# Projections' weights in a stream of their own, two dense chunks between load and split, and one conv buffer for the attention keys

## The chip, the cores and the metric

The kernel runs on one core of a Trainium2 chip. The metric is the device time of one execution in microseconds (us); lower is better. Engines are named as the profile names them: PE is TensorE's matmul and PEld its weight load, DVE is VectorE, ACT is ScalarE, POOL is GpSimd, SP is SyncE, whose queue issues nearly all transfers. A "q" behind an engine's name (SPq) is its instruction queue, where it issues transfers or waits.

## The reference

One encoder block over 2048 tokens and 16 meta tokens of width 1024. One input projection feeds two mixers, whose outputs are joined by an output projection, followed by a SwiGLU feed-forward part.

```python
def reference(x, meta_tokens, g_mix, w_in, ...):
    h = jnp.concatenate([meta, x], axis=1)
    u = rmsnorm(h, g_mix[l])
    proj = u @ w_in[l]
    na_q, na_k, na_v, dn_q, dn_k, dn_v, dn_z, dn_b, dn_a = jnp.split(proj, pts, axis=-1)
    y_na = neighbourhood_attention(na_q, na_k, na_v, na_rel_bias[l], rows)
    y_dn = gated_deltanet(dn_q, dn_k, dn_v, dn_z, dn_b, dn_a, dn_conv_w[l], ...)
    h = h + jnp.concatenate([y_na, y_dn], axis=-1) @ w_out[l]
    u = rmsnorm(h, g_ffn[l])
    h = h + (jax.nn.silu(u @ w_gate[l]) * (u @ w_up[l])) @ w_down[l]
```

`gated_deltanet` first applies a five-tap convolution over the tokens and a silu to q, k and v, then works in chunks of 64 tokens, forward and backward, each of which needs the inverse of a small triangular matrix.

## The kernel before

Three phases follow one another: `phase_a` (the input projection, the convolutions and what the DeltaNet needs before its scan), `phase_b` (attention and scan) and `phase_c` (output projection and feed-forward part). The change lies in `phase_a`, which ends near 890 us of the trace.

All products are kept near f32 accuracy by splitting: a value is `hi`, a rounded copy, plus `lo`, the rest, and a product is three matmuls (hi x hi, hi x lo, lo x hi). A weight tile therefore passes through three steps: a transfer of a raw piece (L220), a cast to `hi` on ACT (L221), a subtraction to `lo` on POOL (L222). The raw pieces share two buffers named `raw`.

`phase_a` goes twice over the units of the projection, once for each half of the tokens. A half has 20 feature units ("f": 12 blocks of DeltaNet channels, 4 pairs of heads of attention keys, 4 of queries; weight tile `wf`, three buffers, two raw pieces each) and 4 natural units ("n": `v0`, `v1`, `z0`, `z1`; tile `wn`, one buffer, four raw pieces). A feature unit is three dense chunks of 24 matmuls at L400, a natural one about eight chunks of 24 at L424. At the end of each chunk stands a tick: the side streams `post` (what follows a convolution), `pre` and `first` (the DeltaNet's chunk work) are Python generators, and each tick moves them to their next `yield`; `yield n` lets n ticks pass. At a unit's start `ahead(u)` writes the loads and splits of units u, u+1 and, where it is a feature unit, u+2.

At the end of a DeltaNet block its convolution is written: the first tap on ACT (L492), four taps on DVE (L494), into a buffer of `ct`, which has two. `post_conv` then makes the silu (Tanh on ACT, L624; product on DVE, L625), lets two ticks pass, and transposes on PE (L631). At the end of an attention key unit, `na_k` makes `hi` (L527, ACT) and `lo` (L528, DVE) of 512 columns twice, each pair in a `ct` buffer of its own, and stores each (L516).

Two loads of results that were stored to memory shortly before stand in `meta_state` (L774, the meta keys `kT`, used by PE at L781) and in `pre_unit` (the inverses' lanes, used by PE at L930). Each engine executes its own list in order; the order in the lists is the program's, with small moves that a scheduler makes.

Of the kernel before, what the change touches and what calls it, by code (L numbers as in the profile page):

```python
# [8 lines left out]
F32 = mybir.dt.float32  # L9
F32R = mybir.dt.float32r  # L10
I32 = mybir.dt.int32
AF = mybir.ActivationFunctionType
ALU = mybir.AluOpType
# [3 lines left out]
P = 128  # L17
NT = 2048
NM = 16
L = NT + NM  # L20
D = 1024
KB = 8
# [3 lines left out]
HT = NT // 2  # L26
# [16 lines left out]
def key_row(r):  # L43
    return r + (r >= 4) + (r >= 27)
# [39 lines left out]
class Side:  # L84
# [8 lines left out]
    def add(self, gen, ready=lambda: True):  # L93
        self.q.append([gen, ready, 0])

    def step(self):
        for e in list(self.q) if self.together else self.q[0:1]:
            if not e[1]():
                continue
            e[2] -= 1  # L100
            if e[2] > 0:
                continue
            try:
                e[2] = next(e[0]) or 1
            except StopIteration:
                self.q.remove(e)
                self.done += 1


class Pieces:  # L110
# [78 lines left out]
def phase_a(tc, S, x, meta, x_t, xe_t, g_mix_b, g_mix_c, w_feat, w_nat0, w_nat, conv_w, a_log, dt_bias, handover):  # L189
# [3 lines left out]
    nc = tc.nc  # L193
    with ExitStack() as es:
        early = es.enter_context(ExitStack())
        cv = early.enter_context(tc.tile_pool(name="cvA", bufs=2))
        wfp = early.enter_context(tc.tile_pool(name="wfA", bufs=3))
        upool = es.enter_context(tc.tile_pool(name="uT", bufs=1, side="right"))
        wpool = es.enter_context(tc.tile_pool(name="wA", bufs=2, side="right"))
# [12 lines left out]
        rb, gb = gb, gb[:, 0:D]  # L212
        gc_ = sm.tile([P, KB], F32, name="gc", bufs=1)
        U = Ctx()
        post, pre, first = Side(True), Side(), Side()
        behind = Behind(tc)

        def split(hi, lo, src):
            raw = wpool.tile(list(src.shape), F32, name="raw")
            nc.sync.dma_start(raw, src)  # L220
            nc.scalar.copy(hi, raw)  # L221
            nc.gpsimd.tensor_tensor(lo, raw, hi, ALU.subtract)  # L222

        def load_feat(b):
            hl = wfp.tile([P, 2, KB, P], F32R, name="wf")
            for q in range(2):
                ks = slice(q * 4, q * 4 + 4)
                split(hl[:, 0, ks], hl[:, 1, ks], w_feat[b][:, ks])
            return hl

        def load_nat(src, n):
            hl = wpool.tile([P, 2, KB, 272], F32R, name="wn", bufs=1)
            for q in range(4):
                ks = slice(q * 2, q * 2 + 2)
                split(hl[:, 0, ks, 0:n], hl[:, 1, ks, 0:n], src[:, ks])
            return hl

        rsx = sm.tile([P, 20], F32, name="rsx", bufs=1)
        nc.gpsimd.memset(rsx, 1.0)
# [126 lines left out]
                    put(job, xt, ci, half, n != 3)  # L366

        def step():
            post.step()
            pre.step()  # L370
            first.step()
# [6 lines left out]
                tick()  # L378

        units, W = [], {}  # L380

        def load(u):
            if u < len(units) and u not in W:
                kind, arg = units[u][0], units[u][1]
                W[u] = load_feat(arg) if kind == "f" else load_nat(*arg)

        def ahead(u):

            load(u)
            load(u + 1)  # L390
            if u + 2 < len(units) and units[u + 2][0] == "f":
                load(u + 2)

        def dense_feat(u, ci, c0, c1):
            hl = W[u]
# [9 lines left out]
        def run_feat(u, ci):  # L405
            kind, b, cols, evac, fin = units[u]
            c0, c1 = cols[ci]
            evac(ci, dense_feat(u, ci, c0, c1))
            tick()
            if ci == 2:  # L410
                fin()
                W.pop(u)

        def run_nat(u, ci):
            kind, (src, n), with_meta, evac, fin = units[u]
            hl = W[u]
            for r0, np_, off, is_meta in U.plan[ci]:
                if np_ == 2 or (is_meta and not with_meta):
                    continue
                ps = pacc.tile([P, 512], F32, name="acc")  # L420
                i = 0
                for k in range(KB):
                    for a, l in ((0, 0), (1, 0), (0, 1)):
                        nc.tensor.matmul(ps[0:np_, 0:n], (U.h, U.l)[l][ci][:, k, off:off + np_], hl[:, a, k, 0:n],  # L424
                                                start=(i == 0), stop=(i == 23))
                        i += 1
                evac(r0 // P, np_, is_meta, ps)
                tick()
            if ci == 2:
                W.pop(u)  # L430
                if fin:
                    fin()

# [65 lines left out]
        def na_k(hp, half):  # L499
            st = Ctx()  # L500
            st.raw = None
            cols = [(16, 400) if half == 0 else (2, 386), (0, 384), (0, 256 if half == 0 else 272)]

            def evac(ci, ps):
                if st.raw is None:
                    st.raw, st.pos = cv.tile([P, HT + NM + 4], F32, name="cr", bufs=3), 0
                n = cols[ci][1] - cols[ci][0]
                nc.scalar.copy(st.raw[:, st.pos:st.pos + n], ps[:, 0:n])
                st.pos += n

            def fin():
                raw = st.raw

                def store(hl, i):
                    n = hl.shape[2]
                    nc.sync.dma_start(S.kx[hp, :, :, :, i * 64:i * 64 + n].rearrange("l a d n -> (a d) l n"), hl.bitcast(F32))  # L516
                if half == 1:
                    m = sm.tile([P, 2, 4, NM], F32R, name="km", bufs=1)
                    mv = bc(raw[:, HT:HT + NM].rearrange("p (o c) -> p o c", o=1), [P, 4, NM])
                    nc.scalar.copy(m[:, 0], mv)  # L520
                    nc.vector.tensor_tensor(m[:, 1], mv, m[:, 0], ALU.subtract)
                    for i in META_ROWS:
                        store(m.rearrange("p l o c -> p l (o c)"), i)
                for rr in range(2):
                    khl = cv.tile([P, 2, 512], F32R, name="ct")
                    g = raw[:, rr * 512:rr * 512 + 512]
                    nc.scalar.copy(khl[:, 0], g)  # L527
                    nc.vector.tensor_tensor(khl[:, 1], g, khl[:, 0], ALU.subtract)  # L528
                    r0 = half * 16 + rr * 8
                    cut = next((c for c in (4, 27) if r0 < c < r0 + 8), r0 + 8)  # L530
                    for c0, c1 in ((r0, cut), (cut, r0 + 8)):
                        if c0 < c1:
                            store(khl[:, :, (c0 - r0) * 64:(c1 - r0) * 64], key_row(c0))
            return ("f", 12 + hp, cols, evac, fin)

        def na_q(hp, half):
# [27 lines left out]
            passes.append(unit_order(half, dn, na, v0, v1, z0, z1))  # L564
        for us in passes:
            units.extend(us)
        u0 = 0
        for pi, us in enumerate(passes):
            if pi == 0:
# [4 lines left out]
            n = len(us)  # L574
# [3 lines left out]
            for gi, grp in enumerate(groups):  # L578
# [4 lines left out]
                if pi == 0 and gi == 13:  # L583
                    first.add(row_rs())
                for i in grp:
                    ahead(u0 + i)
                for ci in range(3):
                    for i in grp:
                        run(u0 + i, ci)
# [170 lines left out]
def meta_state(tc, S, Q, cv, ptp):  # L760

    nc = tc.nc
# [10 lines left out]
    nc.sync.dma_start(gb, bc(S.growm.rearrange("(o h) i -> o h i", o=1), [NM, 4, NM]))  # L773
    nc.sync.dma_start(kT, S.mkT.rearrange("h p i -> p h i"))  # L774
    key_scale(nc, S, slice(0, NM), slice(0, 4), slice(16, 17), False)
    yield 3
    pk_ = ptp.tile([P, 4, P], F32, name="tp").rearrange("p a b -> p (a b)")
    pk = pk_[0:NM, 0:64].rearrange("p (h i) -> p h i", h=4)
    for h in range(4):
# [34 lines left out]
def pre_unit(tc, S, Q, hp, half):  # L814


    nc = tc.nc
    lane = S.lane[hp * 2 + half]
    c0 = half * 8
# [98 lines left out]
    back(ab[32:64, :, 0:32], 1, 1, 1)  # L918
    back(ab[64:96, :, 0:32], 1, 1, 2)
    back(ab[96:128, :, 32:64], 1, 1, 3)  # L920
    yield 4

    def inner(d):

# [972 lines left out]
```

## Time and profile before

| what | value |
|---|---|
| time, median of 3 runs | 2927.22 us (2924.75 to 2933.74) |
| the profiled execution, its own time | 2921.78 us |
| its span in the profile | 2920.1 us |
| PE busy | 2756.5 us (94%) |
| DVE busy | 1780.5 us (61%) |
| ACT busy | 1170.1 us (40%) |
| POOL busy | 745.8 us (26%) |
| mean granted clock of TensorE | 0.966 |

The span is what the profile covers; the time is measured around the whole execution. Busy shares are means over the three phases. Gaps in square brackets in the timeline rows below are the idle time just before an instruction and what ended it.

### The profile page before, as it was taken

To read this page: it belongs to the slowest core of one execution; us is meant where nothing else is said; L and a number is where in the kernel's file an instruction comes from. 1 tells how busy PE (TensorE), PEld (TensorE's weight loads), DVE (VectorE), ACT (ScalarE), POOL (GpSimd) and SP (SyncE) were. 2 spreads that over 40 slices of the span, in tenths; PEclk is the share of its full clock that TensorE was granted. 3 is DMA by queue.
4 is the path that set the end of the run, shared out by engine and by line. 5 is a ranking of instruction groups with operands and counts; after the bars stand their busy time and mean duration, and the time that the engine had idled before them with its cause. 6 is when DMAs were issued, how large, how long until landed. Compare 5 with 4: busy or idle time off the path is not lost.

```text
span 2920.1 us, 45810 instructions
## 1 busy us (share of the span) xinstructions
PE 2756.5 (94%) x16364; PEld 2414.9 (83%) x16364; DVE 1780.5 (61%) x3908; ACT 1170.1 (40%) x2741; POOL 745.8 (26%) x769
## 2 busy tenths in 40 slices
PE   8899989998898998979999999999999999999998
PEld 8889989988888888868887888887887888888886
DVE  5787458796563556874568565555447655554354
ACT  5652233552314666752234233333434332333342
POOL 2353243251421112241224322210014322320010
PEclk9999999999998999989999999999999999999999
DMA  5675564575759988985545222237353222225452
GB/s 160 177 196 147 141 175 122 180 193 148 203 138 281 277 239 236 306 259 182 180 134 182 78 87 82 65 112 262 132 184 111 92 87 78 81 94 193 142 178 73
DMA packets 398017, 466.32 MB, mean 160 GB/s; under 512 B 91955, under 2 KB 302220, under 8 KB 396222
## 3 DMA queue, kind: packets, MB, share of 16 engines
q1 hardware_dynamic: 396062, 457.11, 51.7%
q0 software_dynamic: 1728, 6.29, 0.6%
q8 instruction: 130, 2.13, 0.3%
q14 instruction: 97, 0.79, 0.1%
HBM read 334.14 MB, written 141.15 MB: 163 GB/s over the span
## 4 chain that ended last, share of the span: by engine, by line
PE 68%; DVE 11%; DMA 11%; issue 4%; ACT 2%; POOL 2%; SPq 1%; DVEq 0%; ACTq 0%; POOLq 0%
PE pg L1599 24%; PE pg L1675 8%; PE pd L1459 6%; PE acc L400 4%; PE pd L1675 4%; PE tp L1675 4%; PE acc L424 4%; PE pd L1599 4%; DVE ct L494 2%; PE y L1139 2%; DMA b<-in_rel_dram 2%; DMA qr<-qx 1%; DMA raw<-in_w_nat_dram 1%; DVE tl L162 1%; DVE yl L163 1%
## 5 line engine op out<-in xcount | busy, mean ns | idle before, releaser
L400 PE MATMUL acc<-uh,wf 128*128 128x384 f32 (+5 forms) x1920 | 472.7, 331 | 4.8 <-issue 3.6
L1443 DVE TENSOR_TENSOR w<-rw,w 128x512 fp32r<-128x512 f32 x308 | 244.4, 796 | 250.8 <-ACT w L1442 249.9
L1599 PE MATMUL pg<-T,w 128*128 128x512 f32 x1584 | 393.9, 397 | 1.8 <-ACT T L1442 0.9
L1599 PE MATMUL pg<-B,w 128*128 128x512 f32 x1584 | 389.1, 398 | 3.7 <-ACT B L1442 3.0
L1442 ACT CAST w<-rw 128x512 fp32r<-128x512 f32 x308 | 190.3, 620 | 485.2 <-PE tp L1675 252.2
L1599 PEld LDWEIGHTS pg<-B,w 128*128 128x128 f32 x1584 | 299.8, 190 | 78.0 <-ACT B L1442 4.0
L1599 PEld LDWEIGHTS pg<-T,w 128*128 128x128 f32 x1584 | 298.4, 189 | 75.4 <-ACT T L1442 1.6
L400 PEld LDWEIGHTS acc<-uh,wf 128*128 128x128 f32 x1920 | 342.8, 194 | 3.8 <-ACT uh L335 0.9
L400 PE MATMUL acc<-ul,wf 128*128 128x384 f32 (+5 forms) x960 | 315.1, 328 | 0.6 <-DVE ul L336 0.6
L1675 PE MATMUL pg<-w,hT 128*128 128x512 f32 x1056 | 260.9, 395 | 1.1 <-ACT hT L1442 1.1
L1547 POOL TENSOR_TENSOR s<-rw 128x512 f32<-128x512 f32 x88 | 117.3, 1334 | 548.6 <-DMA rw<-in_w_gate_dram 300.9
L1675 PEld LDWEIGHTS pg<-w,hT 128*128 128x128 f32 x1056 | 198.1, 188 | 49.9 <-ACT hT L1442 1.5
L424 PE MATMUL acc<-wn,uh 128*128 128x256 f32 (+3 forms) x1056 | 209.2, 297 | 6.4 <-DVE vs L468 6.2
L1443 DVE TENSOR_TENSOR w<-s,w 128x512 fp32r<-128x512 f32 x176 | 129.7, 740 | 133.5 <-ACT w L1442 132.3
L1442 ACT CAST w<-s 128x512 fp32r<-128x512 f32 x176 | 108.5, 620 | 234.3 <-PE pg L1599 140.5
L400 PEld LDWEIGHTS acc<-ul,wf 128*128 128x128 f32 x960 | 186.0, 194 | 5.7 <-issue 3.7
L424 PEld LDWEIGHTS acc<-wn,uh 128*128 128x128 f32 (+1 forms) x1056 | 172.5, 196 | 8.8 <-DVE vs L468 6.4
L494 DVE SCALAR_TENSOR_TENSOR ct<-cr,cw,ct 128x1024 f32<-128x1024 f32 (+1 forms) x96 | 140.6, 1467 | 40.4 <-ACT ct L492 38.9
L1459 PE MATMUL pd<-w,yh 128*128 128x512 f32 x512 | 160.0, 394 | 0.0
L424 PE MATMUL acc<-wn,ul 128*128 128x256 f32 (+3 forms) x528 | 156.1, 296 | 2.0 <-DVE rx_i L58 2.0
L222 POOL TENSOR_TENSOR wf<-raw,wf 128x512 fp32r<-128x512 f32 x80 | 110.4, 1396 | 171.7 <-ACT wf L221 154.8
L1613 DVE TENSOR_TENSOR eg<-pg,eg 128x512 f32<-128x512 f32 x110 | 75.9, 690 | 107.2 <-PE pg L1599 107.2
(358 smaller groups left out, 5337.0 us busy)
## 6 DMA issues: line engine op xcount, KB each, us to landing
rw<-in_w_down_dram SPq DMA_DIRECT2D x88, 512.0 KB
rw<-in_w_gate_dram SPq DMA_DIRECT2D x44, 512.0 KB
rw<-in_w_up_dram SPq DMA_DIRECT2D x44, 512.0 KB
hd<-eg SPq DMA_DIRECT2D x88, 256.0 KB
s<-hd SPq DMA_DIRECT2D x88, 256.0 KB
raw<-in_w_feat_dram SPq DMA_DIRECT2D x80, 256.0 KB
w<-dx SPq DMA_DIRECT2D x24, 768.0 KB
xq<-xq SPq DMA_DIRECT2D x32, 512.0 KB
```

The source lines that it names most:

```text
L222: nc.gpsimd.tensor_tensor(lo, raw, hi, ALU.subtract)
L400: nc.tensor.matmul(ps[:, 0:c1 - c0], hl[:, a, k, :], (U.h, U.l)[l][ci][:, k, c0:c1], start=(i == 0), stop=(i == 23))
L424: nc.tensor.matmul(ps[0:np_, 0:n], (U.h, U.l)[l][ci][:, k, off:off + np_], hl[:, a, k, 0:n], start=(i == 0), stop=(i == 23))
L494: nc.vector.scalar_tensor_tensor(tt, raw[:, j:j + T], cw[:, b, j:j + 1], tt, op0=ALU.mult, op1=ALU.add)
L1139: nc.tensor.matmul(po, t.pT[0:w, c], t.v[0:w, c], start=(c == 0), stop=(c == nch - 1))
L1442: nc.scalar.copy(dst_h, src)
L1443: eng.tensor_tensor(dst_l, src, dst_h, ALU.subtract)
L1459: nc.tensor.matmul(ps, (yh, yl)[a][:, k], wo[k][:, b, cs], start=(i == 0), stop=(i == 23))
L1547: nc.gpsimd.tensor_tensor(s, p, q, op)
L1599: nc.tensor.matmul(ps, w[:, a, k], t[:, b, k], start=(k == 0 and (a, b) == (0, 0)), stop=(k == 3 and a == 1))
L1613: nc.vector.tensor_tensor(dst, ps, x0, ALU.add)
L1675: nc.tensor.matmul(acc[j][hf], hk[f][:, a, j * P:(j + 1) * P], wk[f][hf][:, b], start=(f == 0 and i == 0), stop=(f == NFF - 1 and i == 2))
```

## The change

The weights get a side stream `ws` of their own. It steps first at each tick. For each unit it holds a generator that issues a pair of raw transfers, lets two ticks pass, and only then casts and subtracts both. At most three feature tiles and one natural tile are alive; a tile's place is given back at its unit's end (`gone`), and a unit whose weights are not there yet forces the stream on (`load`). `Side.step` therefore takes `force`, and goes on to the next generator in the same tick when one has ended.

`na_k` takes one `ct` buffer of 1024 columns for `hi`; `lo` is written over the raw tile; `hi` and `lo` are stored apart, two row ranges each. The two loads in `meta_state` and `pre_unit` get `yield 5` for `yield 3` and `yield 5` for `yield 4`.

```diff
-    def step(self):
-        for e in list(self.q) if self.together else self.q[0:1]:
+    def step(self, force=False):
+        for e in list(self.q):
             if not e[1]():
-                continue
+                if self.together:
+                    continue
+                return
             e[2] -= 1
-            if e[2] > 0:
-                continue
-            try:
-                e[2] = next(e[0]) or 1
-            except StopIteration:
-                self.q.remove(e)
-                self.done += 1
+            if e[2] <= 0 or force:
+                try:
+                    e[2] = next(e[0]) or 1
+                except StopIteration:
+                    self.q.remove(e)
+                    self.done += 1
+                    continue
+            if not self.together:
+                return
...
-        def split(hi, lo, src):
-            raw = wpool.tile(list(src.shape), F32, name="raw")
-            nc.sync.dma_start(raw, src)
-            nc.scalar.copy(hi, raw)
-            nc.gpsimd.tensor_tensor(lo, raw, hi, ALU.subtract)
...
+        def weights(u):
...
+            for k0 in range(0, KB, 2 * step):
+                raws = []
+                for k in (k0, k0 + step):
+                    raw = wpool.tile([P, step, n], F32, name="raw")
+                    nc.sync.dma_start(raw, src[:, k:k + step])
+                    raws.append((k, raw))
+                yield 2
+                for k, raw in raws:
+                    hi, lo = hl[:, 0, k:k + step, 0:n], hl[:, 1, k:k + step, 0:n]
+                    nc.scalar.copy(hi, raw)
+                    nc.gpsimd.tensor_tensor(lo, raw, hi, ALU.subtract)
+            W[u] = hl
...
         def step():
+            ws.step()
             post.step()
...
-                for rr in range(2):
-                    khl = cv.tile([P, 2, 512], F32R, name="ct")
-                    g = raw[:, rr * 512:rr * 512 + 512]
-                    nc.scalar.copy(khl[:, 0], g)
-                    nc.vector.tensor_tensor(khl[:, 1], g, khl[:, 0], ALU.subtract)
-                    r0 = half * 16 + rr * 8
-                    cut = next((c for c in (4, 27) if r0 < c < r0 + 8), r0 + 8)
-                    for c0, c1 in ((r0, cut), (cut, r0 + 8)):
-                        if c0 < c1:
-                            store(khl[:, :, (c0 - r0) * 64:(c1 - r0) * 64], key_row(c0))
+                hi = cv.tile([P, HT + NM], F32, name="ct")[:, 0:HT].bitcast(F32R)
+                lo = raw[:, 0:HT].bitcast(F32R)
+                nc.scalar.copy(hi, raw[:, 0:HT])
+                nc.vector.tensor_tensor(lo, raw[:, 0:HT], hi, ALU.subtract)
+                r0 = half * 16
+                cut = 4 if half == 0 else 27
+                for c0, c1 in ((r0, cut), (cut, r0 + 16)):
+                    i = key_row(c0)
+                    for l, part in enumerate((hi, lo)):
+                        nc.sync.dma_start(S.kx[hp, l, :, :, i * 64:(i + c1 - c0) * 64].rearrange("a d n -> (a d) n"),
+                                          part[:, (c0 - r0) * 64:(c1 - r0) * 64].bitcast(F32))
...
+        for u, unit in enumerate(units):
+            ws.add(weights(u), lambda u=u, k=unit[0]: u in alive[k] or len(alive[k]) < (3 if k == "f" else 1))
...
-                    ahead(u0 + i)
+                    load(u0 + i)
...
-    yield 3
+    yield 5
...
-    yield 4
+    yield 5
```

What this moves is seen in the order of the instructions. First SP's queue at the end of the first attention key unit, near 125 us of the trace; `kx` is the store of the keys, `raw` a weight's raw piece, `ab` a load for the DeltaNet's decays. Before:

```order
L516 DMA kx_57<-ct_1484 128x2x192
L516 DMA kx_57<-ct_1484 128x2x320
L835 DMA ab_1554<-grow_92 128x256
L220 DMA raw_1626<-in_w_feat_dram 128x512
L220 DMA raw_1630<-in_w_feat_dram 128x512
```

Of the change, at the same place:

```order
L521 DMA kx_57<-km_1475 128x2x64 x2
L538 DMA kx_57<-ct_1480 128x704
L538 DMA kx_57<-ct_1480 128x320
L236 DMA raw_1516<-in_w_feat_dram 128x512
L538 DMA kx_57<-cr_1363 128x704
L538 DMA kx_57<-cr_1363 128x320
L236 DMA raw_1518<-in_w_feat_dram 128x512
```

The second `ct` buffer is gone from the stores, and the pair of raw pieces stands among the stores of one key unit, no longer behind those of a second buffer.

Then ACT's list at the same place: casts of raw pieces, drains of dense chunks (L485, L490 after), the key cast (L527, L531 after) and the first tap of the next convolution (L492, L497 after). Before:

```order
L527 CAST ct_1484<-cr_1372 128x512
L634 ACTIVATE kjunk_1397,kss_1396<-tp_1457 128x128 x4
L634 ACTIVATE kjunk_1397,kss_1396<-tp_1466 128x128 x4
L485 COPY cr_1523<-acc_1567 128x384
L485 COPY cr_1523<-acc_1593 128x256
L221 CAST wf_1625<-raw_1626 128x512
L492 ACTIVATE ct_1619<-cr_1523,cw_154 128x1024
L221 CAST wf_1625<-raw_1630 128x512
```

Of the change:

```order
L531 CAST ct_1480<-cr_1363 128x1024
L642 ACTIVATE kjunk_1393,kss_1392<-tp_1457 128x128 x4
L490 COPY cr_1512<-acc_1487 128x386
L642 ACTIVATE kjunk_1393,kss_1392<-tp_1466 128x128 x4
L490 COPY cr_1512<-acc_1561 128x384
L490 COPY cr_1512<-acc_1587 128x256
L241 CAST wf_1515<-raw_1516 128x512
L241 CAST wf_1515<-raw_1518 128x512
L497 ACTIVATE ct_1617<-cr_1512,cw_154 128x1024
```

The casts now belong to a pair that was issued further ahead, and both stand before the first tap.

Last, ACT's list ahead of the last unit, `z1`: casts of its tile `wn`, drains of query units (L547, L553 after), and the first drain of `z1` itself (L467, L472 after). Before, from the last two of the four casts on:

```order
L221 CAST wn_9633<-raw_9642 128x2x256
L221 CAST wn_9633<-raw_9646 128x2x256
L547 ACTIVATE cr_9390<-acc_9467 128x4x64
L547 ACTIVATE cr_9537<-acc_9512 128x4x96
L547 ACTIVATE cr_9537<-acc_9560 128x4x96
L547 ACTIVATE cr_9537<-acc_9600 128x4x64
L547 ACTIVATE cr_9675<-acc_9650 128x4x96
L547 ACTIVATE cr_9675<-acc_9686 128x4x96
L810 COPY xt_9712<-tp_9681 128x512
L547 ACTIVATE cr_9675<-acc_9715 128x4x64
L467 ACTIVATE vs_9864<-acc_9839 128x256
```

Of the change, from the first of the four on:

```order
L241 CAST wn_9478<-raw_9479 128x2x256
L241 CAST wn_9478<-raw_9481 128x2x256
L553 ACTIVATE cr_9539<-acc_9597 128x4x64
L553 ACTIVATE cr_9650<-acc_9625 128x4x96
L241 CAST wn_9478<-raw_9592 128x2x256
L241 CAST wn_9478<-raw_9594 128x2x256
L553 ACTIVATE cr_9650<-acc_9656 128x4x96
L553 ACTIVATE cr_9650<-acc_9687 128x4x64
L818 COPY xt_9902<-tp_9791 128x512
L472 ACTIVATE vs_9952<-acc_9927 128x256
```

Before, all four casts stand ahead of seven drains of dense chunks; after, the last two stand ahead of two.

## Rows read from the trace of the kernel before

**Rows 1.** One stretch: busy PE, PEld, DVE, ACT, POOL; clock, DMA share, GB/s.

```profile
31.00:890.00 859.00, 782.85 (x6515) 760.94 (x6517) 590.67 (x1370) 344.05 (x924) 294.73 (x331) 0.94 0.60 165
```

**Rows 2.** Waits of PE in 31 to 890: total us, times, longest.

```profile
PE tp L631 <- DVE ct L625: 36.4, 11, 6.1
PE tp L781 <- DMA nat<-mkT: 7.2, 1, 7.2
...
PE pp L930 <- DMA af<-lane: 5.0, 2, 3.9
```

**Rows 3.** Waits of ACT and of SP's queue in 31 to 890.

```profile
ACT wn L221 <- DMA raw<-in_w_nat_dram: 65.1, 20, 11.8
...
ACT wf L221 <- DMA raw<-in_w_feat_dram: 39.4, 18, 7.6
...
ACT ct L527 <- DMA kx<-ct: 11.9, 4, 6.8
SPq L220 <- POOL wf L222: 89.2, 45, 12.6
```

**Rows 4.** Timelines of ACT, SP, DVE and PE, 123 to 146: start, busy us.

```profile
123.48 0.62 ACT L527 CAST ct<-cr 128x512 fp32r<-128x512 f32 x1 [3.36 <-DMA kx<-ct]
125.70 0.89 SPq L516 DMA_DIRECT2D kx<-ct  x2
127.25 3.09 SPq L220 DMA_DIRECT2D raw<-in_w_feat_dram  x2
135.40 0.62 ACT L221 CAST wf<-raw 128x512 fp32r<-128x512 f32 x1 [7.59 <-DMA raw<-in_w_feat_dram]
135.92 1.15 ACT L492 ACTIVATE ct<-cr,cw 128x1024 f32<-128x1024 f32 x1
137.11 6.22 DVE L494 SCALAR_TENSOR_TENSOR ct<-cr,cw,ct 128x1024 f32<-128x1024 f32 x4 [6.58 <-ACT ct L492]
145.17 1.11 PE L631 MATMUL tp<-ident,ct 128*128 128x128 f32 x4 [6.09 <-DVE ct L625]
```

**Rows 5.** Timelines of ACT and PE around 390, 660 and 716.

```profile
389.41 0.62 ACT L221 CAST wf<-raw 128x512 fp32r<-128x512 f32 x1 [5.21 <-DMA raw<-in_w_feat_dram]
391.98 0.75 PE L631 MATMUL tp<-ident,ct 128*128 128x128 f32 x4 [4.04 <-DVE ct L625]
658.39 0.66 PE L631 MATMUL tp<-ident,ct 128*128 128x128 f32 x4 [0.56 <-DVE ct L625]
714.04 0.62 ACT L221 CAST wn<-raw 128x512 fp32r<-128x512 f32 x1 [11.81 <-DMA raw<-in_w_nat_dram]
716.71 0.66 PE L631 MATMUL tp<-ident,ct 128*128 128x128 f32 x2 [5.39 <-DVE ct L625]
```

**Rows 6.** The chain that ended last, in order of time: start, us, what.

```profile
130.01 5.93 DMA raw<-in_w_feat_dram
213.31 9.88 PE acc L424 x83
223.19 11.49 PE acc L400 x72
699.84 14.17 DMA raw<-in_w_nat_dram
```

**Rows 7.** Groups by line and shape, 31 to 890: busy, mean ns, idle before.

```profile
L528 DVE TENSOR_TENSOR ct<-cr,ct 128x512 fp32r<-128x512 f32 x16 | 14.0, 873 | 8.9 <-ACT ct L527 8.9
L222 POOL TENSOR_TENSOR wf<-raw,wf 128x512 fp32r<-128x512 f32 x76 | 105.4, 1402 | 169.0 <-ACT wf L221 152.1 <-PE tp L631 10.6 <-PE pp L864 5.9
L222 POOL TENSOR_TENSOR wn<-raw,wn 128x512 fp32r<-128x512 f32 x24 | 36.3, 1517 | 58.5 <-ACT wn L221 53.6 <-DMA raw<-in_w_nat_dram 5.0
```

**Rows 8.** Timelines of POOL and DVE, 463 to 467.

```profile
463.32 2.84 POOL L222 TENSOR_TENSOR wf<-raw,wf 128x512 fp32r<-128x512 f32 x2 [1.83 <-ACT wf L221]
463.62 1.40 DVE L163 TENSOR_TENSOR yl<-yl,tl 128x255 f32<-128x255 f32 x1
466.48 0.42 DVE L163 TENSOR_TENSOR yl<-yl,tl 128x256 f32<-128x256 f32 x1
```

More of the change, by code (lines that the diff above doesn't have):

```diff
@@ L214, in phase_a @@
         U = Ctx()
-        post, pre, first = Side(True), Side(), Side()
+        post, pre, first, ws = Side(True), Side(), Side(), Side()
         behind = Behind(tc)
-        def split(hi, lo, src):
-            raw = wpool.tile(list(src.shape), F32, name="raw")
-            nc.sync.dma_start(raw, src)
-            nc.scalar.copy(hi, raw)
-            nc.gpsimd.tensor_tensor(lo, raw, hi, ALU.subtract)
[L224 to L236, printed above, removed]
+        def weights(u):
+            kind, arg = units[u][0], units[u][1]
+            if kind == "f":
+                hl = wfp.tile([P, 2, KB, P], F32R, name="wf")
+                n, step, src = P, 4, w_feat[arg]
+            else:
+                src, n = arg
+                hl, step = wpool.tile([P, 2, KB, 272], F32R, name="wn", bufs=1), 2
+            alive[kind].add(u)
+            for k0 in range(0, KB, 2 * step):
[10 more added lines that the diff above has]
+            W[u] = hl
         rsx = sm.tile([P, 20], F32, name="rsx", bufs=1)
@@ L380, in phase_a, with gone @@
         units, W = [], {}
+        alive = {"f": set(), "n": set()}
         def load(u):
[L383 to L392, printed above, removed]
+            while u not in W:
+                ws.step(True)
+        def gone(u):
+            W.pop(u)
+            alive[units[u][0]].discard(u)
         def dense_feat(u, ci, c0, c1):
@@ L411, in run_feat @@
                 fin()
-                W.pop(u)
+                gone(u)
         def run_nat(u, ci):
@@ L429, in run_nat @@
             if ci == 2:
-                W.pop(u)
+                gone(u)
                 if fin:
```

## The prediction

> **What bounds the kernel now.** I read first the busy time by stretch. Of the 859 us between 31 and 890, the projections' stage, TensorE works 782.85 us and is idle 76 [rows 1]; no other engine passes 591. So the stage is held by TensorE, and the change can win there only what TensorE idles, unless it makes TensorE wait for something new. Outside that stretch the two programs issue nearly the same TensorE rows in the same order, so I expect nothing there.
>
> Then the list of what TensorE waits for in that stretch [rows 2]: 36.4 us in eleven waits of the conv transposes (L631) for VectorE's silu (L625), 7.2 us in one wait for the meta keys' load (L781), 5.0 us in two waits for the lane loads (L930), together 48.6 us. No wait for a weight tile is in that list: `wf` and `wn` reach TensorE in time. The rest of the 76 us is many small waits and issue time that the change does not address.
>
> Weights nevertheless show up one step upstream. ScalarE waits 65.1 us in 20 waits at the cast L221 for raw rows of `w_nat` and 39.4 us in 18 for `w_feat`, 104.5 together; SP waits 89.2 us for GpSimd's split to free a raw buffer [rows 3]. ScalarE executes in order, so whatever is queued behind such a cast waits too. The question is how many of the eleven TensorE waits begin there.
>
> Three do, and I followed each back by time. At 145.17 TensorE has waited 6.09 us for L625. The silu comes after the five-tap conv, whose taps on VectorE (L494, from 137.11, 6.22 us in all) had waited 6.58 us for ScalarE's first tap L492 (135.92), and that stood behind a cast (135.40) that had waited 7.59 us for its raw weights. Those were only issued at 127.25, because on SP they stand behind the key store of the second `ct` buffer, whose cast L527 (123.48) had itself waited 3.36 us for an earlier key store to leave the buffer [rows 4]. At 391.98 (4.04 us) and 716.71 (5.39 us) it is shorter: the silu's Tanh L624 comes directly behind a cast that waited 5.21 us (389.41) and one that waited 11.81 us (714.04) [rows 5]. Sum of the three: 6.09 + 4.04 + 5.39 = 15.5 us.
>
> **The change, part by part.**
>
> *The casts no longer stand right behind their loads.* Before, load, cast and split of a weight are written in one go at a unit's start. After, a pair of loads is written, then two dense chunks pass, then the two casts and splits. A feature chunk takes 11.49/72 x 24 = 3.83 us, a natural one 9.88/83 x 24 = 2.86 us [rows 6], so the cover is 7.7 or 5.7 us. Raw loads that something waited for took some 6 us (5.93 at 130.01) and, once, 14.17 us [rows 6]. So most waits of a cast end, and for the three gaps I take 12 of the 15.5 us: about 1.2 us stays in each, because after the cast the chain of L492, four taps, silu still has to run, and the smallest gap of this kind, with no late cast ahead of it, is 0.56 us [rows 5]. Bounds: 0 and 15.5.
>
> *The other eight waits* sum to 36.4 - 15.5 = 20.9 us. Ahead of them VectorE is late too, but by mixed causes: casts that waited earlier for weights, the key units' `ct` pair, and VectorE's own queue with the inversion (L162, L163) between the taps. I take half, 10.4; bounds 0 and 20.9, no row decides between them.
>
> *The attention keys.* One 1024-wide cast and one 1024-wide subtraction replace two of each 512 wide, and `lo` is written over the raw tile; so a key unit takes one `ct` buffer and not two, and the 11.9 us that L527 waits for key stores [rows 3] should go. Its worth in TensorE time lies in the gap at 145 already counted. VectorE's part was 16 x 873 ns = 14 us [rows 7] and cannot become more than that. Four stores go out per unit instead of three, 8 more in all; two of them held SP for 0.89 us [rows 4], and SP has waits of 89 us to lose. I cost it at nothing, under cover of SP's idle time; without the cover it is 8 x 0.5 = 4 us.
>
> *The yields.* The meta keys' load gets two more ticks before its products. In program order the distance grows only from 0.42 to 0.96 of a chunk, since ticks in the last groups pass without dense work: 0.54 x 2.86 = 1.5 us of the 7.2. The lane loads' distance to L930 is the same in both orders, though a dense chunk now stands between L930's products and what follows. I take 4 of 7.2 + 5.0 = 12.2; bounds 1.5 and 12.2.
>
> *What the new distance costs.* The same two chunks come off the other side. Counted in program order from a tile's last split to TensorE's first use, a feature unit had about 5 chunks in hand (3.5 to 14) and now has about 2; a natural one had 3.6 to 6.3 and now has 0.8 to 2.0; two units of the second half (`v0` and the fourth conv block) have none. The rows of ScalarE before `z1` show it: all four casts of `wn` ahead of seven drains before, the last two with two drains behind them after. If one load is as late as the 14.17 us one, it lies 14.17 - 5.7 = 8.5 us past its cover, less a reserve of about one chunk of 2.86, some 6 us of TensorE; the two units without reserve cost about a split (1.5 us, [rows 7]) each. I take 9; bounds 0 (the list before has no such wait) and 28 (seven of the eight natural units late by 4 us each, a landing of 14 against cover and reserve being rare, one of 6 to 10 not).
>
> **Sum.** -12 - 10.4 - 4 + 9 = -17.4 us. The profiled execution took 2921.8 us (span 2920.1), so 2904.4; it stands 5.4 us under the median of the runs shown, 2927.2, and so I forecast 2909.8, **2910**. Its own range, with 5 us either way on the eight waits and 6 on the late weights, is about 8 us either way, 2902 to 2918.
>
> **The rivals.**
>
> *VectorE is late for a reason that stays (2924).* The transposes wait for VectorE, and the 100 splits on GpSimd in the stretch are as many and as long as before: 105.4 + 36.3 us [rows 7]. A subtraction of VectorE's inversion, 128 x 255, took 1.40 us at 463.62 beside a pair of splits running from 463.32 for 2.84 us, and one of 128 x 256 took 0.42 us at 466.48, after them [rows 8]. If such stretching makes the silu late, moving the splits by two chunks only moves the collision. By the rows: a third of the 22.4 us of the first two terms remains (7.5), the yields give 4, the new distance costs 9, so -3: 2924. Against it: in the three largest gaps the step before is an idle ScalarE, not a stretched VectorE. The Trainium skill, "SBUF — State Buffer", section "Who interferes with whom", says that a DVE instruction with two SBUF inputs and a GpSimd instruction that reads SBUF exclude one another; the trace agrees (1.40 against 0.42), and the taps and the silu have two such inputs. By that rule alone none of the first 22.4 us would come, and the time would be about 2932.
>
> *Weights arrive late (2942, slower).* The place is the start of the natural units: TensorE at L429 (the old L424) behind the last split of `wn`. It decides when a pair's casts come more than about 2.5 us after their turn, which is what one nat chunk of reserve leaves after a split; before, 20 such casts waited 65.1 us, 3.3 us each on average, and the longest 11.81. Seven units by 4 us are 28, half of the 26.4 us of gains still comes (13), so +15: 2942. Against it: half of those 3.3 us are covered by the two chunks, and TensorE waits for no weight before.
>
> *All of it closes (2878).* The eleven waits, the meta keys' and the lanes' go, and no weight is late: 48.6 us less, 2878.6. For it: every one of these waits ends with VectorE or a load, and both have time to spare. Against it: the smaller waits have no cast ahead of them.
>
> **How the numbers follow.** Chances: forecast 0.53, VectorE late anyway 0.25, late weights 0.16, all closes 0.06. A difference of 0.3%, 8.8 us, is what a measurement of this kernel can tell from no change. The forecast and the last case are faster by more, 0.59; the first rival lies within it, 0.25; the second is slower, 0.16. Leaving out the second rival's upper part and the last case, the range is 2888 (the forecast with the eight waits gone whole and no late weight, 2890, and 2 us more of the three gaps) to 2932 (the first rival with nothing of the first two terms).
>
> **What would show it.** The casts' waits for raw fall from 104.5 to under 40 us; TensorE's waits for the silu fall from 36.4 to about 14; the meta keys' wait falls from 7.2 to about 5. If the casts' waits fall and TensorE's waits for the silu do not, the first rival is right. If TensorE waits for `wf` or `wn` appear in the list with more than 15 us, the second is. I am wrong, too, if the time moves outside 31 to 890.

## The result and the profile after

The changed kernel takes 2906.51 us (median of 5 runs, 2900.0 to 2912.7) against 2927.35 for the kernel before: ratio 0.9925, interval 0.9903 to 0.9947. The forecast was 2910 in 2888 to 2932. The profiled execution has a span of 2898.0 us, 22.1 less than before.

Where the time came from is read by stage. The windows below end with the last dense chunk of the projections' stage; columns are the window, its length, then busy time (and count) of PE, PEld, DVE, ACT, POOL, then granted clock, share of the transfer engines, GB/s. First the kernel before:

```profile
31.00:898.50 867.50, 791.35 (x6599) 769.17 (x6600) 592.21 (x1373) 346.00 (x928) 298.22 (x333) 0.94 0.61 166
```

The changed kernel:

```profile
31.00:884.00 853.00, 788.46 (x6602) 765.59 (x6603) 588.06 (x1367) 347.13 (x924) 305.53 (x334) 0.95 0.62 169
```

The stage is 14.5 us shorter. TensorE's idle time in it is 11.6 us less (76.15 before, 64.54 now), and its busy time 2.9 us less, at a granted clock of 0.95 and not 0.94. The other 7.6 us lie behind the stage. There the two kernels issue the same matmuls, but not all in the same order. A second profile of the same changed kernel (run again below) is 2.8 us longer there than the first, so part of those 7.6 us is spread; I do not claim them for the change. In the kernels below the time behind the stage goes from 2010 to 2033 us, though no experiment edits a line of it. A difference in the whole time is therefore not yet a difference in the stage, and the stage's end is given with the ratio where it matters.

TensorE's waits in 31 to 890 after (total us, times, longest), the answer to [rows 2]:

```profile
PE tp L639 <- DVE ct L633: 15.9, 9, 4.0
PE pp L938 <- DMA af<-lane: 11.5, 3, 6.3
PE acc L429 <- DVE vs L473: 10.3, 2, 7.5
...
PE acc L405 <- POOL wf L242: 0.9, 1, 0.9
...
PE tp L789 <- DMA nat<-mkT: 0.6, 1, 0.6
```

The silu waits fell from 36.4 to 15.9 us and the meta keys' from 7.2 to 0.6, together 27.1. The lanes' waits rose, from 5.0 to 11.5, and so did the products of a natural unit that wait for VectorE to drain the one before (L429, L424 before), from 6.2 to 10.3. This is most of why 27.1 us less of the first two came to only 11.6 us less idle time. A wait for a weight is now there, but it is one of 0.9 us. ScalarE's waits for raw pieces, against [rows 3]:

```profile
ACT wf L241 <- DMA raw<-in_w_feat_dram: 28.0, 19, 4.0
ACT wn L241 <- DMA raw<-in_w_nat_dram: 26.6, 10, 7.6
```

They halved, from 104.5 to 54.6 us. The largest gap of before [rows 4] is gone, as the same place shows in the timelines of ScalarE and TensorE (start, busy us, in brackets the idle time just before):

```profile
130.66 0.62 ACT L241 CAST wf<-raw 128x512 fp32r<-128x512 f32 x1 [2.25 <-DMA raw<-in_w_feat_dram]
132.47 0.62 ACT L241 CAST wf<-raw 128x512 fp32r<-128x512 f32 x1 [1.19 <-DMA raw<-in_w_feat_dram]
133.00 1.15 ACT L497 ACTIVATE ct<-cr,cw 128x1024 f32<-128x1024 f32 x1
...
141.35 0.66 PE L639 MATMUL tp<-ident,ct 128*128 128x128 f32 x4 [0.31 <-DVE ct L633]
```

The cast ahead of the first tap waits 2.25 us and not 7.59, and the transposes wait 0.31 us and not 6.09. The other two gaps that the prediction followed back, 4.04 us at 392 and 5.39 us at 717, are gone altogether: TensorE's list after has no wait for the silu between 284 and 462 us and none behind 661. So 15.2 of the 15.5 us of these three gaps went, and the other eight waits fell from 20.9 to 15.6 us.

### The profile page after: what moved, and what is told of

The parts are those of the page before. It is cut to its first block, busy times and chain, and to the rows that moved or that the text cites. A ratio compares the mean times of both kernels' runs of the same rounds, so it can differ in the third digit from the quotient of the medians.

```text
span 2898.0 us, 45796 instructions
## 1 busy us (share of the span) xinstructions
PE 2750.9 (95%) x16364; PEld 2407.7 (83%) x16364; DVE 1772.8 (61%) x3900; ACT 1170.8 (40%) x2733; POOL 754.4 (26%) x769
## 4 chain that ended last, share of the span: by engine, by line
PE 53%; DVE 3%; DMA 2%; issue 1%; ACT 1%; POOL 0%; SPq 0%; DVEq 0%; ACTq 0%; POOLq 0%
PE pg L1607 24%; PE pg L1683 8%; PE pd L1467 6%; PE pd L1683 4%; PE tp L1683 4%; PE pd L1607 4%; PE y L1147 1%; DVE z L1284 1%; PE tp L1420 0%; DVE w L1451 0%; PE tp L1493 0%; DMA b<-in_rel_dram 0%; DMA k<-kx 0%; POOL s L1555 0%; PE y L1133 0%
## 5 line engine op out<-in xcount | busy, mean ns | idle before, releaser
L429 PE MATMUL acc<-wn,uh 128*128 128x256 f32 (+3 forms) x1056 | 209.9, 298 | 10.6 <-DVE vs L473 10.3
L429 PEld LDWEIGHTS acc<-wn,uh 128*128 128x128 f32 (+1 forms) x1056 | 172.6, 197 | 13.8 <-DVE vs L473 10.7
L242 POOL TENSOR_TENSOR wf<-raw,wf 128x512 fp32r<-128x512 f32 x80 | 119.6, 1509 | 157.7 <-ACT wf L241 134.5
L429 PE MATMUL acc<-wn,ul 128*128 128x256 f32 (+3 forms) x528 | 157.4, 298 | 2.4 <-DVE rx_i L58 2.4
```

## The experiments

Twelve kernels were run, one of them the changed kernel again. Every ratio is to the kernel before, timed on the same chip beside it.

**One part at a time.** The stream alone:

```diff
 # the changed kernel, but na_k as before, and
-    yield 5
+    yield 3
...
-    yield 5
+    yield 4
```

> The changed kernel with the old attention keys (two ct buffers a unit) and the old yields (3 and 4): the weight stream alone. If the gain is the casts that no longer stand in front of the silu (my theory), this alone gives most of it: ratio to the kernel before 0.993 to 0.996, the casts' waits for raw pieces near 55 us as in the changed kernel, PE's waits for the silu 15 to 22 us. If the gain lies in the keys' single ct buffer (rival A), it is within 0.2% of the kernel before and PE's waits for the silu stay above 30 us.

The attention keys alone, in the kernel before:

```diff
-                for rr in range(2):
-                    khl = cv.tile([P, 2, 512], F32R, name="ct")
...
+                hi = cv.tile([P, HT + NM], F32, name="ct")[:, 0:HT].bitcast(F32R)
+                lo = raw[:, 0:HT].bitcast(F32R)
```

> The kernel before with only the attention keys changed (one ct buffer, lo over the raw tile). My theory: only the 6 us gap at 145 us goes or shrinks, ratio 0.997 to 1.000, PE's waits for the silu about 30 us. Rival A (the keys carry the gain): ratio 0.993 to 0.995.

The yields alone, in the kernel before:

```diff
-    yield 3
+    yield 5
...
-    yield 4
+    yield 5
```

> The kernel before with only the two yields changed (3 to 5 and 4 to 5). My theory: 1.5 to 7 us less, ratio 0.9975 to 0.9995; PE's 7.2 us wait for the meta keys shrinks. Rival B (the yields carry a third of the gain or more): ratio 0.996 to 0.997 with both the meta keys' and the lanes' waits gone.

Stream and keys, with the old yields (3 and 4):

> The changed kernel with the old yields: stream and keys. My theory: ratio 0.993 to 0.996, within 5 us of the changed kernel; the 7.2 us wait for the meta keys is back, the lanes' waits stay about 11 us, since one yield more does not change what stands between the lanes' store and their loads. Rival B: 7 us or more slower than the changed kernel.

Measured: stream alone 0.9965 (0.9949 to 0.9982); keys alone 1.0004 (0.9987 to 1.0022); yields alone 1.0062 (1.0043 to 1.0082); stream and keys 0.9897 (0.9878 to 0.9915). So the stream is what lowers the silu waits: 16.6 us with it alone, 42.4 with the keys alone. Stream and keys together give more than their sum, by 21 us. The yields cost time by themselves; in the change the two intervals still overlap (0.9878 to 0.9915 without them, 0.9903 to 0.9947 with them), and this is taken up below.

The expectations did worse than the forecast. The stream's ratio lies just outside its range; its silu waits are as expected. The keys' ratio lies just above theirs, and the silu waits rose to 42.4 us where I had expected about 30. The yields lost where a gain was expected. Stream and keys came out below their range, the meta keys' wait did not come back, and the lanes' waits were 3.4 us and not 11.

TensorE's waits in 31 to 890 with the stream alone:

```profile
PE tp L638 <- DVE ct L632: 16.6, 7, 4.4
PE pp L937 <- DMA af<-lane: 13.6, 3, 9.0
```

and with the keys alone:

```profile
PE tp L632 <- DVE ct L626: 42.4, 10, 8.0
```

With the yields alone the loss lies at the end of the stage. The windows hold the same last 16 of its 186 dense chunks. With the yields 47 other matmuls are not in it (802 and not 849); they run behind the last dense chunk. First the kernel before, then the yields:

```profile
817.00:898.00 81.00, 73.84 (x849) 70.83 (x848) 36.80 (x89) 15.26 (x31) 16.06 (x14) 0.94 0.66 167
```

```profile
817.00:911.00 94.00, 81.41 (x802) 77.10 (x800) 44.41 (x112) 15.50 (x33) 17.45 (x16) 0.82 0.58 144
...
880.00:900.00 20.00, 16.31 (x384) 15.22 (x383) 5.95 (x11) 4.07 (x8) 2.30 (x3) 0.76 0.73 183
900.00:920.00 20.00, 18.26 (x141) 16.93 (x140) 3.97 (x10) 3.81 (x9) 5.22 (x6) 0.50 0.59 180
```

The window takes 94 us and not 81: 5.4 us more idle time (12.6 against 7.2) and 7.6 us more busy time for fewer matmuls, at a granted clock of 0.82 and not 0.94. TensorE was idle 3.7 of the 20 us ahead of 900 with the clock already falling, and then ran 20 us at 0.50, the lower of its two levels (1.2 GHz). Which of the two yields did this in the kernel before was not tried.

**Which yield costs in the changed kernel.** Three kernels on one chip: the changed kernel again; with the meta keys' yield back at 3; with the lanes' back at 4.

> The changed kernel itself, as the base for the other three on the same chip. Ratio to the kernel before 0.990 to 0.995, as measured first (0.9925).

```diff
 # meta_state
-    yield 5
+    yield 3
```

> The changed kernel with the meta keys' yield back at 3; the lanes' yield stays 5. Theory L (the longer wait for the lanes is what the yields cost, since in the run with old yields PE's waits for the lanes fell from 11.5 to 3.4 us): within 4 us of the changed kernel, lanes' waits about 10 us. Theory M (the longer meta keys' wait costs it, by ticks in the drain without dense work): about 15 us faster than the changed kernel.

```diff
 # pre_unit
-    yield 5
+    yield 4
```

> The changed kernel with the lanes' yield back at 4; the meta keys' yield stays 5. Theory L: 8 to 15 us faster than the changed kernel, near the 0.990 of stream and keys alone, lanes' waits about 3 us. Theory M: within 4 us of the changed kernel.

Measured: 0.9927 (0.9908 to 0.9947), 0.9933 (0.9911 to 0.9956) and 0.9904 (0.9887 to 0.9922). Undoing the meta keys' yield changes nothing that is measured, undoing the lanes' gives some 7 to 8 us (2902.37 to 2894.34 in the medians; the intervals overlap a little). Theory L holds, at the low end of its range, but a longer distance as such should not lengthen the wait for the same transfer. What does is seen on SP. The changed kernel, SP's timeline, with TensorE's first product behind it:

```profile
678.62 2.67 SPq L465 DMA_DIRECT2D vx<-vn  x4
681.33 0.58 SPq L905 DMA_DIRECT2D lane<-yl  x1
683.40 0.34 SPq L907 DMA_DIRECT2D lane<-ul  x1
701.75 1.97 SPq L916 DMA_DIRECT2D U<-lane  x4
...
705.82 0.31 PE L938 MATMUL pp<-af,U 32*32 32x32 f32 x2 [6.27 <-DMA af<-lane]
```

The kernel with the lanes' yield at 4, the same place:

```profile
667.33 0.33 SPq L905 DMA_DIRECT2D lane<-yl  x1
...
670.03 1.40 SPq L916 DMA_DIRECT2D U<-lane  x3
...
674.65 0.65 SPq L465 DMA_DIRECT2D vx<-vn  x1
```

`vx<-vn` are four copies of the values inside memory, 2 x 1088 and 2 x 816 KB, 3.8 MB, which the second value unit issues when it ends. With yield 4 the lanes' store goes out ahead of them and its loads follow 2.7 us later. With yield 5 the store comes behind them; SP's next load waits 18.0 us for it, and TensorE 6.27 us. Between these two kernels one tick decided the order. It is not so in general: in the kernel before, with yield 4, the store stood behind the copies too.

```profile
688.60 2.67 SPq L460 DMA_DIRECT2D vx<-vn  x4
691.32 0.47 SPq L897 DMA_DIRECT2D lane<-yl  x1
...
SPq L908 <- DMA lane<-yl: 13.9, 3, 10.2
```

The copies are also not where most of the difference arises. Counted by dense chunks, the kernel with the lanes' yield at 4 ends the stage 13.3 us earlier (870.7 against 884.0 us). From the 103rd to the 120th chunk it gains 8.3 us, more than 100 us ahead of the copies; from the 145th to the 156th, where copies and lanes stand, 5.5. Both stretches, first of the changed kernel, then with yield 4:

```profile
458.40:561.10 102.70, 91.88 (x932) 88.14 (x931) 70.18 (x171) 49.66 (x161) 25.73 (x25) 0.92 0.57 165
670.40:739.50 69.10, 62.44 (x747) 59.61 (x746) 30.93 (x57) 16.05 (x29) 11.08 (x11) 0.93 0.59 171
```

```profile
455.50:549.90 94.40, 87.40 (x933) 84.00 (x932) 69.19 (x172) 49.49 (x160) 26.22 (x25) 0.96 0.64 186
661.20:724.80 63.60, 62.12 (x751) 59.23 (x750) 27.59 (x50) 17.72 (x34) 15.24 (x16) 0.97 0.74 203
```

In the first stretch the four kernels with stream and yield 5 (the changed one twice, meta yield 3, and the next run) take 102.0 to 104.7 us; the four with stream, yield 4 and the splits as they are (stream alone, stream and keys, lanes' yield 4, and three ticks below) take 93.3 to 95.9. In each of the first four a cast waits some 4 us for its raw piece, and TensorE 3.4 to 3.8 us behind it; in the other four TensorE has no wait of 1 us there for VectorE's `nat` copies. The changed kernel:

```profile
470.76 0.62 ACT L241 CAST wf<-raw 128x512 fp32r<-128x512 f32 x1 [4.03 <-DMA raw<-in_w_feat_dram]
472.88 0.69 DVE L644 COPY nat<-tp 128x512 f32<-128x512 f32 x1 [3.08 <-ACT kjunk L642]
473.62 0.66 PE L639 MATMUL tp<-ident,ct 128*128 128x128 f32 x4 [3.54 <-DVE nat L644]
```

That is the prediction's own mechanism, at a place that one tick moved. How the tick makes this load late was not followed. Behind the stage the kernel with yield 4 loses again (2024.8 against 2014.0 us), so that the time shows less than the 13.3 us.

> The changed kernel (yields 5 and 5) in which the four copies of the values (vn to vx, 3.8 MB) that end the second value unit do not run at that place; four copies of the first four heads' values run instead behind those of the first value unit, so that heads 4 to 7 read the wrong values. Theory of the queue (with five ticks the lanes' store of the third chunk unit comes just behind these copies, and SP's lane loads then wait 18 us): SP's wait for the lanes' store falls from 18 to under 5 us, PE's 6 us wait for the lanes goes, and the kernel is 5 to 10 us faster than the changed one: ratio 0.989 to 0.991. Theory of the tick (one tick more is a longer chain by itself): within 3 us of the changed kernel.

```diff
-                for C in range(4):
-                    nc.sync.dma_start(S.vx[C][h0:h0 + 4].rearrange("h r c d -> h r (c d)"),
+                for C, d0 in [(C, d0) for d0 in (0, 4) for C in range(4)]:
+                    nc.sync.dma_start(S.vx[C][d0:d0 + 4].rearrange("h r c d -> h r (c d)"),
...
-            v1 = ("n", (w_nat[0], 256), half == 0, evac_v(4, 0), None if half else fin_v(4))
+            v1 = ("n", (w_nat[0], 256), half == 0, evac_v(4, 0), None)
```

This kernel copies the values of heads 4 to 7 before they are there; only its time is of use. Measured: 0.9885 (0.9869 to 0.9902), by the ratios some 12 us under the changed kernel's 0.9927. The waits do what the theory of the queue says: SP's longest wait for the lanes' store is 2.2 us (18.0 before), and TensorE waits 0.4 us for the lanes.

```profile
SPq L916 <- DMA lane<-yl: 8.3, 4, 2.2
```

The time, however, does not come from there:

```profile
31.00:881.90 850.90, 790.14 (x6601) 766.35 (x6601) 588.05 (x1364) 346.31 (x920) 307.81 (x333) 0.95 0.61 169
```

The stage ends at 881.9 us, only 1.2 to 2.1 us ahead of the changed kernel's two profiles (883.1 and 884.0). The stretch of the copies is 66.4 us long and not 69.1 or 70.0; the earlier stretch, 102.0 us, is as slow as in the changed kernel. The rest of the gain lies behind the stage, where attention and scan, with their instructions in another order, take 423.8 us against 430.2 and 433.1. The kernel with three ticks, the next one below, copies the values as usual and has such a short phase too (425.1). So the copies' place is worth some 3 us in its own stretch, and the 12 us are not shown to be its work.

In that stretch alone the kernels sort themselves by the order. With the copies ahead of the lanes' store or around it, those with the stream take 69.1 to 73.3 us; with the lanes first, or the copies early, 63.6 to 68.4. With the stream alone, where the copies stand around the store, TensorE's longest wait for the lanes was 9.0 us. Of the 21.3 us by which stream and keys end the stage ahead of the stream alone (866.5 against 887.8), 7.8 arise in that stretch (64.0 against 71.8).

**How near to the use the weights may come.** Stream and keys, old yields, three ticks:

```diff
-                yield 2
+                yield 3
                 for k, raw in raws:
```

> Stream and keys with the old yields, with three ticks between load and split and not two. In program order the last splits of the natural tiles then fall up to 1.6 chunks after the tile's first product, and those of eight feature units 0.2. Rival of late weights: the cliff lies here: PE waits for wn and wf appear with 20 us or more and the kernel is 20 us or more slower than stream and keys alone (ratio 1.000 or above), while the casts' waits for raw pieces fall below 30 us. If the distance does not matter: ratio 0.987 to 0.992 as with two ticks.

Measured: 0.9887 (0.9870 to 0.9904), the same as with two ticks. ScalarE waits 27.4 us for raw pieces (41.2 with two ticks), and the waits for weights do come up in TensorE's list, but they are small:

```profile
PE acc L405 <- ACT wf L241: 2.7, 4, 1.0
...
PE acc L429 <- POOL wn L242: 2.2, 3, 1.1
PE acc L405 <- POOL wf L242: 2.0, 4, 1.5
PE acc L429 <- ACT wn L241: 1.6, 2, 1.3
```

They sum to 8.5 us in 13 waits. The whole time loses nothing that is measured, but the stage does:

```profile
31.00:883.50 852.50, 791.39 (x6602) 766.50 (x6601) 581.26 (x1366) 347.81 (x921) 302.00 (x334) 0.95 0.61 169
```

It ends 17.0 us later than with two ticks (866.5, the first row of the next experiment), with 7.1 us more idle time of TensorE; the changed kernel's two profiles lie 0.9 us apart. Behind the stage the kernel is 8.4 us shorter (2012.1 against 2020.5). So no cliff of 20 us shows in the time within one tick of the change, but the third tick is not free where the weights are used.

**Do POOL's splits hold VectorE?** Each split executed twice, in stream and keys with the old yields:

```diff
                     nc.gpsimd.tensor_tensor(lo, raw, hi, ALU.subtract)
+                    nc.gpsimd.tensor_tensor(lo, raw, hi, ALU.subtract)
```

> Stream and keys with the old yields, in which each of POOL's 112 split subtractions is executed twice (same result, some 140 us more POOL work in the stage). Theory of the casts: POOL's splits hardly matter while lo is in time, 0 to 8 us slower than stream and keys alone. Rival (VectorE is held by the splits): DVE's taps and inversion stretch, PE's waits for the silu rise from 19 to 30 us or more and the time by 15 us or more.

Measured: 1.0267 (1.0248 to 1.0286), about 108 us more than the 0.9897 without the doubling. My theory's 0 to 8 us was wrong by far and the rival's mechanism is real. The stage, first with each split once, then twice:

```profile
31.00:866.50 835.50, 781.50 (x6600) 758.78 (x6601) 590.36 (x1362) 345.68 (x920) 308.25 (x333) 0.96 0.63 172
```

```profile
31.00:968.00 937.00, 812.88 (x6646) 783.80 (x6645) 678.22 (x1367) 350.08 (x932) 462.11 (x445) 0.92 0.56 155
```

POOL works 154 us more; VectorE, whose instructions are the same, is busy 88 us longer, and the stage is 101 us longer. Late weights are not what makes it: TensorE's waits for a doubled split sum to 4.3 us. The kernel before shows the same in single instructions: of the inversion's sixteen operations of L163 on 128x252 and 128x255, the two that ran beside a split took 1.40 us, the other fourteen 0.40 to 0.43 (one of the two is in [rows 8]). The taps of 1024 columns, first once, then twice (busy, mean ns):

```profile
L499 DVE SCALAR_TENSOR_TENSOR ct<-cr,cw,ct 128x1024 f32<-128x1024 f32 x48 | 69.2, 1447 | 16.3 <-ACT ct L497 15.6
```

```profile
L500 DVE SCALAR_TENSOR_TENSOR ct<-cr,cw,ct 128x1024 f32<-128x1024 f32 x48 | 78.3, 1636 | 17.7 <-ACT ct L498 17.2
```

So the other way was tried, the splits on VectorE:

```diff
-                    nc.gpsimd.tensor_tensor(lo, raw, hi, ALU.subtract)
+                    nc.vector.tensor_tensor(lo, raw, hi, ALU.subtract)
```

> Stream and keys with the old yields, with the 112 split subtractions on DVE and not on POOL. If POOL's splits stretch DVE's work by more than the subtractions cost DVE itself (112 by about 0.7 us, 78 us; doubling them on POOL cost 108 us): 5 to 15 us faster than stream and keys alone, ratio 0.985 to 0.988. If what matters is DVE's own load and order: 5 to 20 us slower, ratio 0.991 to 0.997.

Measured: 0.9821 (0.9803 to 0.9840), 2875.05 us, faster than even that theory had it (0.985). The stage and two groups:

```profile
31.00:857.50 826.50, 780.88 (x6602) 761.47 (x6602) 575.67 (x1470) 347.54 (x925) 157.56 (x229) 0.95 0.63 173
```

```profile
L499 DVE SCALAR_TENSOR_TENSOR ct<-cr,cw,ct 128x1024 f32<-128x1024 f32 x48 | 64.7, 1353 | 8.4 <-ACT ct L497 8.0
...
L242 DVE TENSOR_TENSOR wf<-raw,wf 128x512 fp32r<-128x512 f32 x75 | 53.3, 725 | 16.7 <-ACT wf L241 16.6
...
L242 DVE TENSOR_TENSOR wn<-raw,wn 128x512 fp32r<-128x512 f32 x24 | 16.3, 691 | 16.2 <-ACT wn L241 16.1
```

VectorE took over some 100 subtractions, at 725 ns where POOL needed about 1500, and is busy 14.7 us less than without them (575.67 against 590.36). TensorE's waits for the silu fall to 6.4 us, from 18.9. By the ratios the gain is some 22 us; in the two profiles the stage is 9.0 us shorter.

In that kernel the lanes came behind the copies again, and SP waited 17.6 us. The last run issues the copies on POOL's queue:

```diff
-                    nc.sync.dma_start(S.vx[C][h0:h0 + 4].rearrange("h r c d -> h r (c d)"),
+                    nc.gpsimd.dma_start(S.vx[C][h0:h0 + 4].rearrange("h r c d -> h r (c d)"),
```

> The kernel with the splits on DVE (stream and keys, old yields), with the copies of the values (vn to vx) issued on POOL's queue and not on SP's. In the run before this one SP again waited 17.6 us for the lanes' store, which stood right behind these copies. If the queue's order makes that wait: it falls under 8 us, PE's 13.8 us of waits for the lanes under 7, and the ratio goes from 0.982 to 0.978 to 0.981. If the copies' share of the transfer engines makes it, whoever issues them: the wait stays above 12 us and the ratio within 0.2% of 0.982.

Measured: 0.9816 (0.9796 to 0.9837), 2868.07 us. SP's longest wait for the store falls to 6.8 us and TensorE's waits for the lanes from 13.8 to 6.0 us, so the queue's order made most of the wait. The stretch from the 145th to the 156th chunk takes 62.2 us and not 72.3. In the whole time the gain is too small to be told from none.

```profile
SPq L916 <- DMA lane<-yl: 8.6, 2, 6.8
```

The last two kernels beat both the kernel before and the changed one.

## Why the prediction was right, and where it was not

**The three gaps and the eight waits** (-12 and -10.4, 22.4 together): the silu waits fell by 20.5 us, and with the stream alone by nearly as much. This was the right mechanism at nearly the right size. By place, 15.2 us came from the three gaps, more than the 12 taken, and 5.3 from the other eight, half of what was taken. The step below it was over-stated: the casts' waits were to fall under 40 us and fell to 54.6. Half was enough, since a cast that waits 2 us delays the taps by little.

**The attention keys** (nothing): this term was mis-sized. Alone they give nothing measurable, as costed; with the stream they give 0.9965 to 0.9897, some 20 us. Of the 21.3 us in the stage, 5.8 arise in the six chunks behind the first key unit (24.5 against 30.3 us): with the stream alone L532, the key cast, still waited 5.4 us for a store at 126 us, and the gap behind it was 2.9 us. Another 7.8 arise where copies and lanes stand. What the single `ct` buffer does to the rest was not separated.

**The yields** (-4): this step failed in its sign. It priced the distance between a load and its use, chunk by chunk, and left out what else a tick moves: a late raw load in front of a cast at 470 us, and the lanes' store behind 3.8 MB of copies on SP (where it also stood in the kernel before). The meta keys' wait did go, but it is as small with the old yield once the stream is there (it is not in TensorE's list of stream and keys), so the new yield bought nothing. The lanes' yield costs some 7 to 8 us of the time; of the 13.3 us in the stage, 8.3 lie ahead of the copies and 5.5 at them. The order of SP's queue around the copies was to be had beforehand, and the prediction looked at another place of it.

**Weights nearer to their use** (+9): too large. It is 0.9 us in TensorE's list; casts wait up to 7.6 us for a raw piece, and hardly any of it reaches TensorE as a wait for a weight. The second rival (2942) is refuted for this distance. One tick further the stage does pay, 17.0 us.

So the forecast's 2910 against 2906.5 owes its closeness to luck. By the ratios the stream alone gave 10 us, where its terms (-12, -10.4, +9) say 13.4; the keys, put at nothing, gave 20 more; the yields, put at a gain of 4, took back 8. The three errors (3.4 us less, 20 more, 12 less) largely cancelled. The prediction had also said that it is wrong if the time moves outside the stage, and 7.6 of the 22.1 us between the two profiles did; the forecast of 17.4 us less in the stage stands against 14.5.

**VectorE is late for a reason that stays** (2924): as a forecast wrong, as a mechanism right, and cheaper to dismiss than it should have been. The splits do hold VectorE, for more than the change gains; but the stretch is about the same before and after (the taps of 1024 columns take 1546 ns before and 1494 after), so it was no reason against the change's own gain. My argument that ScalarE and not VectorE stood idle in the three largest gaps was right for these gaps and said nothing on the rest: the other eight waits lost only a quarter, and it was moving the splits that brought all silu waits down to 6.4 us. The Trainium skill, "SBUF — State Buffer", section "Who interferes with whom", gives the exclusion as a rule. These runs agree with it in direction, and show the price in this stage: 88 us of VectorE for 154 us of POOL.

**All of it closes** (2878): did not happen in the changed kernel; the kernel with the splits on VectorE takes about that time (2875.05), by another way.

## What to carry to other kernels

Split load and use of a streamed operand when a cast in an in-order queue is what waits for the load: here half of the casts' waits went, and with them more than half of TensorE's waits behind them. Before you lengthen a yield, print the order of every queue around the moved step, and look for a large copy next to a small round trip through memory. When a wait has gone, look whether the stage ends earlier, and by how much: the copies' 6 us wait went and the stage gained 2 us at most, and three ticks cost the stage 17 us that the whole time does not show. Where GpSimd and VectorE both do two-operand work in the same stretch, count GpSimd's time as VectorE's too, and try the work on VectorE.

## What the runs showed of the hardware

Moving some 100 subtractions to an engine that was already busy 590 of 835 us made it less busy. Beside POOL's splits VectorE's other work took some 87 us longer: 590.36 us against 575.67 less the 72.5 us of subtractions taken over. That is the same price as the other way round, where 154 us more of splits on POOL made VectorE 88 us busier.

With four copies of 3.8 MB ahead of a 512 KB store on the same queue, the next load waited 18.0 us for the store (10.2 in the kernel before); with the store ahead of the copies 2.2 to 3.3 us, and with the copies on another queue 6.8. The Trainium skill, "DMA: Bandwidth & Descriptors", section "Queues, rings and completion order", says that each transfer engine takes turns between the queues it has work for, and takes one queue's work in order; the waits agree with it.

Idle time in TensorE came with slower work: in the yields' run 5.4 us more idle in a stretch stood beside 7.6 us more busy time for the same dense chunks and 47 other matmuls fewer, at a clock of 0.82 against 0.94.
